# Attention phases of a two-layer encoder: TensorE kept in the order of the code, and projection steps spread 1.3 : 0.1 : 1.7

## The chip, the cores and the metric

The kernel runs on one NeuronCore of one Trainium2 chip. The metric is device time in microseconds (us) of one launch. Of the kernel before, three runs are shown: 2111.12, 2111.41 and 2112.37 us, so the median is 2111.41 us.

## The reference, cut to what matters

Two layers are computed over 1024 tokens of width 1024. The token mixer differs (windowed attention with 12 query heads and 4 key/value heads in layer 0, neighbourhood attention with 12 heads in layer 1); beside it, each layer has 4 heads of cross-attention into 256 memory tokens.

```python
for i in range(DEPTH):                       # DEPTH = 2
    h = rmsnorm(x, norm_mix[i])
    proj = h @ (w_in_a if i % 2 == 0 else w_in_b)      # q, k, v, q_mem
    y_tok = windowed_gqa(q, k, v, sink) if i % 2 == 0 else neighbourhood_attn(q, k, v, rpb)
    y_mem = softmax(q_mem @ k_mem^T * 64**-0.5) @ v_mem
    x = x + concat(y_tok, y_mem) @ w_out[i]
    h = rmsnorm(x, norm_ffn[i])
    gu = h @ w_gate_up[i]
    x = x + (silu(gu[..., :D_FF]) * gu[..., D_FF:]) @ w_down[i]
return rmsnorm(x, norm_final)
```

Every product is made of three fp32r matmuls (high x high, high x low, low x high), which is why each operand is split into a high and a low part.

## The kernel before, in words

**What the attention phase consists of.** Each layer has 16 heads (12 token heads and 4 memory heads), and each head is worked on in two halves of 512 queries, so there are 32 halves, in the order memory heads 0 and 1, token heads 0 to 5, memory heads 2 and 3, token heads 6 to 11. Below, half 0 is the first of a layer. A half (class `Half`, L713) has three jobs:

- `scores` (L739): four query blocks of 128. For each, two matmuls (K high, K low) write a PSUM bank named S; then VectorE and ScalarE read it. For a token head, VectorE adds the bias and takes the maximum in one instruction (L758), which frees the bank, and ScalarE makes the exponential (L762). For a memory head, VectorE takes the maximum (L753) and ScalarE reads the same bank for the exponential (L754), so the bank is free only after both. At the end GpSimd scales the four blocks p (L776).
- `turn` (L784): for each of the four blocks two or three transpositions on TensorE into a PSUM bank named pT (L791), which ScalarE and VectorE copy out as a high part ph and a low part pl (L107 and L110, helpers that serve all splits).
- `mix` (L800): 4 or 10 matmuls on ph and pl into the one bank O (L812), which ScalarE and VectorE copy into y (L822, L833).

PSUM has two banks for S, three that pT shares with the transpositions of V (`vtr`, L596), one for O, and two for the projections (mm, po). So the third block of a half's scores waits until the first block's bank has been read, and the fourth transposed block until the first one's has been copied.

**The projections between.** The input projections of the heads to come are units of two halves of 8 steps (`other_units`, L894); a step is one call of `pull` and issues three 512-column matmuls (L141). After the last unit the same calls bring steps of the output projection, with the tile po (`out_units`, L948). The main loop (L966) goes over the halves. In round i it traces `scores` of half i+1, `mix` of half i-1 and `turn` of half i, and after each block it adds rate/13 to a credit; each whole credit is one `pull`. The rate is what the most urgent unit needs to be done half a round before it is due; once the units are done, it is read from PACE (L37): 0, 2, 4, 4, 4 for the last five rounds.

**What sets the order.** The code is traced in one order, but the instructions of each engine are then put in order by a scheduler, which may move a matmul ahead of others that are traced before it when it reckons that one to be ready sooner. Softmax work and the copies of pT are raised in priority; projection steps are not. So the order in which the code writes TensorE's work is not the one that it runs in.

## Time and profile before

| what | value |
|---|---|
| median of three runs | 2111.41 us |
| the profiled execution's own time | 2112.72 us |
| its span, first to last instruction | 2110.9 us |
| TensorE, matmul busy | 2092.0 us, 99% of the span |
| TensorE, weight loads busy | 1751.5 us, 83% |
| VectorE busy | 1524.3 us, 72% |
| ScalarE busy | 1076.9 us, 51% |
| GpSimd busy | 582.7 us, 28% |

The two attention phases lie at about 75 to 320 us (layer 0) and 1040 to 1390 us (layer 1) of the span; the rest is the memory projections and the feed-forward parts, which the change does not touch. In the profile PE is TensorE's matmul row and PEld its weight loads, DVE is VectorE, ACT ScalarE, POOL GpSimd, SP SyncE. Each matmul has its own weight load. The busy time of a matmul is longer than the distance to the next one's start, since matmuls are pipelined; the distance between starts is what a matmul costs in a stream. In the views by source line the idle time before an instruction is put down to what ended it; "issue" is idle time that ends with no such event.

### The profile page before, as it was taken

To read this page: it belongs to the slowest core of one execution; us is meant where nothing else is said; L and a number is where in the kernel's file an instruction comes from. 1 tells how busy PE (TensorE), PEld (TensorE's weight loads), DVE (VectorE), ACT (ScalarE), POOL (GpSimd) and SP (SyncE) were. 2 spreads that over 40 slices of the span, in tenths; PEclk is the share of its full clock that TensorE was granted. 3 is DMA by queue.
4 is the path that set the end of the run, shared out by engine and by line. 5 is a ranking of instruction groups with operands and counts; after the bars stand their busy time and mean duration, and the time that the engine had idled before them with its cause. 6 is when DMAs were issued, how large, how long until landed. Compare 5 with 4: busy or idle time off the path is not lost.

```text
span 2110.9 us, 29032 instructions
## 1 busy us (share of the span) xinstructions
PE 2092.0 (99%) x10318; PEld 1751.5 (83%) x10318; DVE 1524.3 (72%) x2474; ACT 1076.9 (51%) x2037; POOL 582.7 (28%) x615
## 2 busy tenths in 40 slices
PE   9999999999999999999999999999999999999998
PEld 8788888888888888888888888888788888888886
DVE  7787886897666666866766666677986666678675
ACT  6687785544334335444466666664543434344443
POOL 0344330334434430000233223203343444400001
PEclk9999999999999999999999999999999999999999
DMA  6421138232333227956232222274233333277562
GB/s 233 146 82 51 31 103 283 89 115 101 109 115 110 85 105 281 337 180 206 80 98 68 69 72 78 65 269 155 75 110 105 110 115 105 91 263 280 184 210 94
DMA packets 121776, 288.07 MB, mean 136 GB/s; under 512 B 12704, under 2 KB 21152, under 8 KB 121632
## 3 DMA queue, kind: packets, MB, share of 16 engines
q1 hardware_dynamic: 113744, 272.42, 38.5%
q10 hardware_dynamic: 7888, 13.79, 1.7%
q8 instruction: 82, 1.34, 0.3%
q14 instruction: 62, 0.51, 0.1%
HBM read 211.19 MB, written 68.95 MB: 133 GB/s over the span
## 4 chain that ended last, share of the span: by engine, by line
PE 80%; issue 12%; DVE 3%; POOL 2%; ACT 2%; DMA 1%; SPq 0%; POOLq 0%; ACTq 0%; DVEq 0%
PE X L1104 16%; PE Y L1104 16%; PE mm L141 15%; PE po L141 8%; PE X L1542 5%; PE Y L1542 4%; PE S L746 3%; PE O L812 3%; PE pT L791 3%; PE X L1186 2%; PE Y L1186 2%; PE mm L448 1%; POOL wS L1061 1%; POOL wf L110 1%; DVE wgu L110 0%
## 5 line engine op out<-in xcount | busy, mean ns | idle before, releaser
L1104 PE MATMUL Y<-hB,wgu 128*128 128x512 f32 x1056 | 255.6, 391 | 0.8 <-ACT c L1124 0.8
L1104 PE MATMUL X<-hB,wgu 128*128 128x512 f32 x1056 | 254.9, 391 | 0.0
L1542 PE MATMUL X<-hB,wd 128*128 128x512 f32 (+1 forms) x1092 | 242.9, 383 | 0.0
L110 DVE TENSOR_TENSOR wgu<-wS,wgu 128x1024 fp32r<-128x1024 f32 (+1 forms) x124 | 154.3, 1245 | 120.5 <-ACT wgu L107 120.4
L1542 PEld LDWEIGHTS X<-hB,wd 128*128 128x128 f32 x1092 | 200.2, 188 | 40.1 <-issue 0.5
L1104 PEld LDWEIGHTS Y<-hB,wgu 128*128 128x128 f32 x1056 | 196.8, 188 | 43.4 <-ACT c L1124 1.6
L1104 PEld LDWEIGHTS X<-hB,wgu 128*128 128x128 f32 x1056 | 195.9, 188 | 40.1 <-ACT g L1121 0.2
L776 POOL TENSOR_SCALAR p<-p,stat 128x384 f32<-128x384 f32 (+1 forms) x256 | 141.8, 573 | 302.5 <-DVE stat L773 196.7
L141 PE MATMUL mm<-hT,wqk 128*128 128x512 f32 x672 | 199.2, 405 | 0.0
L107 ACT CAST wgu<-wS 128x1024 fp32r<-128x1024 f32 (+1 forms) x124 | 114.3, 923 | 141.9 <-POOL wS L1061 124.5
L141 PE MATMUL po<-yT,wo 128*128 128x512 f32 x768 | 183.5, 394 | 0.0
L1542 PE MATMUL Y<-hB,wd 128*128 128x512 f32 x792 | 180.2, 389 | 0.0
L1542 PEld LDWEIGHTS Y<-hB,wd 128*128 128x128 f32 x792 | 148.7, 188 | 30.8
L244 POOL TENSOR_TENSOR nr<-nv,neg_half 128x4 f32<-128x4 f32 (+1 forms) x12 | 13.2, 1103 | 582.6 <-DVE nv L243 573.3
L141 PEld LDWEIGHTS po<-yT,wo 128*128 128x128 f32 x768 | 142.9, 188 | 29.1 <-DVE yT L110 0.2
L107 ACT CAST hB<-b_raw 128x512 fp32r<-128x512 f32 x154 | 89.7, 618 | 124.9 <-DMA b_raw<-b_d 108.0
L1104 PE MATMUL X<-hT,wgu 128*128 128x512 f32 x624 | 150.3, 391 | 0.0
L1061 POOL TENSOR_TENSOR wS<-wgu_raw 128x512 f32<-128x512 f32 x44 | 61.1, 1389 | 291.6 <-DVE wgu L110 291.6
L1104 PEld LDWEIGHTS X<-hT,wgu 128*128 128x128 f32 x624 | 116.9, 188 | 26.2
L762 ACT ACTIVATE p<-p,stat 128x256 f32<-128x256 f32 (+1 forms) x192 | 112.3, 586 | 48.7 <-DVE stat L758 47.1
L110 DVE TENSOR_TENSOR hB<-b_raw,hB 128x512 fp32r<-128x512 f32 x154 | 100.3, 689 | 49.8 <-ACT hB L107 49.6
L110 DVE TENSOR_TENSOR pl<-pT,ph 128x384 fp32r<-128x384 f32 (+1 forms) x256 | 119.2, 493 | 17.5 <-ACT ph L107 14.3
(201 smaller groups left out, 4248.3 us busy)
## 6 DMA issues: line engine op xcount, KB each, us to landing
wgu_raw<-in_w_gu SPq DMA_DIRECT2D x92, 512.0 KB, 3.6
b_raw<-b_d SPq DMA_DIRECT2D x70, 512.0 KB, 4.5
wd_raw<-in_w_dn SPq DMA_DIRECT2D x50, 512.0 KB, 4.5
b_d<-c SPq DMA_DIRECT2D x88, 256.0 KB, 2.1
b_d<-t SPq DMA_DIRECT2D x66, 256.0 KB, 2.2
wo_raw<-in_w_out SPq DMA_DIRECT2D x32, 512.0 KB, 3.7
wd_other<-in_w_dn SPq DMA_DIRECT2D x20, 512.0 KB, 7.3
xr_d<-x ACTq DMA_DIRECT2D x32, 256.0 KB, 2.9
```

The lines of the kernel that those rows point to most:

```text
L107: return nc.scalar.copy(dst, src)
L110: return (eng or nc.vector).tensor_tensor(dst, src, h.bitcast(F32), op=ALU.subtract)
L141: nc.tensor.matmul(ps[:, :n], l, r, start=start and i == 0 and j == 0, stop=stop and i == len(order) - 1 and j == 2,)
L746: nc.tensor.matmul(s_[:, :n], Q[self.h][:, qb * P : (qb + 1) * P], k, start=j == 0, stop=j == 1)
L762: nc.scalar.activation(p[:, :n], p[:, :n], AF.Exp, bias=m1, scale=-1.0, accum_out=s1)
L776: nc.gpsimd.tensor_scalar(p[:, :n], p[:, :n], ri[:, i : i + 1], 1.0, op0=ALU.mult, op1=ALU.mult)
L791: nc.tensor.transpose(tr[:, j * P : (j + 1) * P], p[:, j * P : (j + 1) * P], ident)
L812: nc.tensor.matmul(o[:, c0 : c0 + w * P], self.value(j), t[:, s0 : s0 + w].rearrange("p j q -> p (j q)"), start=j == js[0] and t is self.p ...
L1061: sub = lambda o, p_, q_: nc.gpsimd.tensor_tensor(o, p_, q_, op=ALU.subtract)
L1104: nc.tensor.matmul(ps, l, r, start=n in (0, 1, 3, 6) and k == 0 and i == 0, stop=k == 3 and i == 2, skip_group_check=True,)
L1186: nc.tensor.matmul(bank[:, at : at + h2], l, r, start=start and k == 0 and i == 0, stop=stop and k == 1 and i == 2, skip_group_check=True,)
L1542: nc.tensor.matmul(bank[:, c], l, r, start=i in (0, 1, 3, 6) and p == 0 and n == 0, stop=p == HF - 1 and n == 2, skip_group_check=True,)
```

## The change

Three things are changed, all in the attention phases. First, while the main loop runs (a flag `in_order`), every TensorE instruction of the projections, scores, transpositions and mixes is pinned behind the TensorE instruction traced before it. Pinning sets the order of issue only; it adds no wait for a result. Second, the credit that a block adds is weighted by its job: 1.3 for a block of `scores`, 0.1 for a step of `mix`, 1.7 for a block of `turn`. Third, the rate aims a little earlier: 0.7 in place of 0.5 rounds before the due round, with a floor of 0.4 in place of 0.5. No arithmetic and no transfer is added or removed; the number of matmuls of each kind is the same.

```diff
--- before.py
+++ after.py
@@ -138,11 +138,16 @@
         for i, k in enumerate(order):
             terms = three(wk(w, k), (h[k][:, 0, :n], h[k][:, 1, :n]))
             for j, (l, r) in enumerate(terms):
-                nc.tensor.matmul(
+                pe(nc.tensor.matmul(
                     ps[:, :n], l, r, start=start and i == 0 and j == 0,
                     stop=stop and i == len(order) - 1 and j == 2,
-                )
+                ))
             yield
+
+    in_order = [False]
+
+    def pe(ins):
+        return tc.keep_in_program_order(ins) if in_order[0] else ins
 
     def run(g):
         for _ in g:
@@ -593,7 +598,7 @@
                     tr = ps_t.tile([P, HS], F32, tag="T", name="vtr")
                     for b in range(4):
                         c = (4 * u + b) * P
-                        nc.tensor.transpose(tr[:, b * P : (b + 1) * P], vt[:, c : c + P], ident)
+                        pe(nc.tensor.transpose(tr[:, b * P : (b + 1) * P], vt[:, c : c + P], ident))
                     for i in range(2):
                         s_ = tr.rearrange("p (b i d) -> p b i d", b=4, i=2)[:, :, i]
                         hi(vs[i][:, 4 * u : 4 * u + 4, 0], s_)
@@ -743,9 +748,9 @@
                     for i, (qb, b0, b1, n) in enumerate(self.blocks):
                         s_ = ps_s.tile([P, HS], F32, tag="S", name="S")
                         for j, k in enumerate(self.keys(b0, b1)):
-                            nc.tensor.matmul(
+                            pe(nc.tensor.matmul(
                                 s_[:, :n], Q[self.h][:, qb * P : (qb + 1) * P], k, start=j == 0, stop=j == 1
-                            )
+                            ))
                         p = ap.tile([P, 3 * P], F32, tag="p", bufs=8, name="p")
                         m1, s1 = nm[:, i : i + 1], sm[:, i : i + 1]
                         with tc.high_priority(offset=40):
@@ -788,7 +793,7 @@
                     for p, (qb, b0, b1, n) in zip(self.p, self.blocks):
                         tr = ps_t.tile([P, HS], F32, tag="T", name="pT")
                         for j in range(b1 - b0):
-                            nc.tensor.transpose(tr[:, j * P : (j + 1) * P], p[:, j * P : (j + 1) * P], ident)
+                            pe(nc.tensor.transpose(tr[:, j * P : (j + 1) * P], p[:, j * P : (j + 1) * P], ident))
                         s0 = self.slot(b0, qb)
                         sl = slice(s0, s0 + step * (b1 - b0 - 1) + 1, step)
                         src = tr[:, :n].rearrange("p (j q) -> p j q", q=P)
@@ -809,12 +814,12 @@
                         s0, w = self.slot(j, qbs[0]), len(qbs)
                         c0 = (qbs[0] - 4 * u) * P
                         for t in (self.ph, self.pl):
-                            nc.tensor.matmul(
+                            pe(nc.tensor.matmul(
                                 o[:, c0 : c0 + w * P], self.value(j),
                                 t[:, s0 : s0 + w].rearrange("p j q -> p (j q)"),
                                 start=j == js[0] and t is self.ph, stop=j == js[-1] and t is self.pl,
                                 skip_group_check=True,
-                            )
+                            ))
                         yield
 
                     t = temp("yt")
@@ -963,6 +968,7 @@
                 if is_a:
                     pull()
             groups = 13
+            in_order[0] = True
             for i in range(len(halves)):
 
                 rate = 0.0
@@ -970,7 +976,7 @@
                     if done[0] > n:
                         continue
                     left = (n + 1 - n0) * 2 * NK - taken[0]
-                    rate = max(rate, left / max(dues[n] - i - 0.5, 0.5))
+                    rate = max(rate, left / max(dues[n] - i - 0.7, 0.4))
                 if tail is not None:
                     rate = PACE[layer][i - len(halves)]
                 if i == 0:
@@ -981,16 +987,16 @@
                         spread_bias(r)
                 jobs = []
                 if i + 1 < len(halves):
-                    jobs.append(halves[i + 1].scores())
+                    jobs.append((1.3, halves[i + 1].scores()))
                 ahead = halves[min(i + 3, len(halves) - 1)].h
                 if not isinstance(ahead, tuple) and ahead not in biases:
                     biases[ahead] = make_bias(ahead)
                 if i > 0:
-                    jobs.append(halves[i - 1].mix())
-                jobs.append(halves[i].turn())
-                for job in jobs:
+                    jobs.append((0.1, halves[i - 1].mix()))
+                jobs.append((1.7, halves[i].turn()))
+                for share, job in jobs:
                     for _ in job:
-                        credit += rate / groups
+                        credit += share * rate / groups
                         while credit >= 1.0:
                             credit -= 1.0
                             pull()
@@ -1001,6 +1007,7 @@
                 at[0] = i + 1
                 if done[0] == len(units) and tail is None:
                     tail = work = out_units()
+            in_order[0] = False
             for _ in halves[-1].mix():
                 pull()
             run(tail)
```

Line numbers of the changed kernel are higher: the scores are L751 there, the transpositions L796, the mixes L817. A name ends in the number of its tile. Three places on TensorE follow.

Layer 0, the scores of half 17 (second half of memory head 2): the two banks are used in turn by the blocks S_2423, S_2429, S_2438 and S_2444. Before:

```order
L746 MATMUL S_2423<-mKL_1646,QS_1643 128x256
L746 MATMUL S_2429<-mKH_1645,QS_1643 128x256
L746 MATMUL S_2429<-mKL_1646,QS_1643 128x256
L141 MATMUL mm_2398<-hT_586,wv_1804 128x512 x3
L812 MATMUL O_2455<-ph_2379,V_833 128x128
L812 MATMUL O_2455<-pl_2380,V_833 128x128
L141 MATMUL mm_2398<-hT_624,wv_1804 128x512
L746 MATMUL S_2438<-mKH_1645,QS_1643 128x256
L746 MATMUL S_2438<-mKL_1646,QS_1643 128x256
L141 MATMUL mm_2398<-hT_624,wv_1804 128x512
L746 MATMUL S_2444<-mKH_1645,QS_1643 128x256
L746 MATMUL S_2444<-mKL_1646,QS_1643 128x256
```

The same half in the changed kernel, where the blocks are S_2426, S_2435, S_2441 and S_2450:

```order
L751 MATMUL S_2426<-mKH_1593,QS_1591 128x256
L751 MATMUL S_2426<-mKL_1594,QS_1591 128x256
L141 MATMUL mm_2385<-hT_624,wv_1760 128x512 x3
L751 MATMUL S_2435<-mKH_1593,QS_1591 128x256
L751 MATMUL S_2435<-mKL_1594,QS_1591 128x256
L751 MATMUL S_2441<-mKH_1593,QS_1591 128x256
L751 MATMUL S_2441<-mKL_1594,QS_1591 128x256
L141 MATMUL mm_2385<-hT_629,wv_1760 128x512 x3
L751 MATMUL S_2450<-mKH_1593,QS_1591 128x256
L751 MATMUL S_2450<-mKL_1594,QS_1591 128x256
```

Before, the first two blocks are followed by three projection matmuls, two of a mix and one more before the third block. Now the first block is followed by one step of three, then the second and the third block stand back to back, and the third has one step and the second block between it and the block whose bank it takes.

Layer 0, the end of the phase: the transpositions of half 26 (their end, before) and the scores of half 28. Before:

```order
L791 MATMUL pT_3445<-ident_106,p_3305 128x128 x3
L141 MATMUL po_3548<-yT_3269,wo_3254 128x512
L746 MATMUL S_3454<-KH_2838,QS_3104 128x256
L746 MATMUL S_3454<-KL_2839,QS_3104 128x256
L746 MATMUL S_3460<-KH_2838,QS_3104 128x384
L746 MATMUL S_3460<-KL_2839,QS_3104 128x384
L141 MATMUL po_3548<-yT_3269,wo_3254 128x512
L141 MATMUL po_3548<-yT_3274,wo_3254 128x512 x2
L746 MATMUL S_3466<-KH_2838,QS_3104 128x384
L746 MATMUL S_3466<-KL_2839,QS_3104 128x384
L141 MATMUL po_3548<-yT_3274,wo_3254 128x512
L746 MATMUL S_3472<-KH_2838,QS_3104 128x384
```

The same place in the changed kernel:

```order
L796 MATMUL pT_3424<-ident_106,p_3287 128x128 x2
L796 MATMUL pT_3433<-ident_106,p_3293 128x128 x3
L796 MATMUL pT_3439<-ident_106,p_3302 128x128 x3
L796 MATMUL pT_3445<-ident_106,p_3308 128x128 x3
L751 MATMUL S_3454<-KH_2809,QS_3115 128x256
L751 MATMUL S_3454<-KL_2810,QS_3115 128x256
L751 MATMUL S_3460<-KH_2809,QS_3115 128x384
L751 MATMUL S_3460<-KL_2810,QS_3115 128x384
L751 MATMUL S_3466<-KH_2809,QS_3115 128x384
L751 MATMUL S_3466<-KL_2810,QS_3115 128x384
L751 MATMUL S_3472<-KH_2809,QS_3115 128x384
L751 MATMUL S_3472<-KL_2810,QS_3115 128x384
```

Before, steps of the output projection (po) stand between these blocks; now the four transposed blocks and the four blocks of scores follow each other with nothing between.

Layer 1, the scores of half 13, of a token head. Before:

```order
L746 MATMUL S_11129<-KH_10590,QS_10589 128x384
L746 MATMUL S_11129<-KL_10591,QS_10589 128x384
L141 MATMUL mm_11070<-hT_9631,wqk_10674 128x512 x3
L746 MATMUL S_11138<-KH_10590,QS_10589 128x384
L746 MATMUL S_11138<-KL_10591,QS_10589 128x384
L141 MATMUL mm_11160<-hT_9357,wqm_10861 128x512 x3
L746 MATMUL S_11164<-KH_10590,QS_10589 128x384
L746 MATMUL S_11164<-KL_10591,QS_10589 128x384
L746 MATMUL S_11170<-KH_10590,QS_10589 128x256
L746 MATMUL S_11170<-KL_10591,QS_10589 128x256
```

The same half in the changed kernel:

```order
L751 MATMUL S_11161<-KH_10515,QS_10514 128x384
L751 MATMUL S_11161<-KL_10516,QS_10514 128x384
L141 MATMUL mm_11136<-hT_9413,wqm_10815 128x512 x3
L751 MATMUL S_11170<-KH_10515,QS_10514 128x384
L751 MATMUL S_11170<-KL_10516,QS_10514 128x384
L141 MATMUL mm_11136<-hT_9418,wqm_10815 128x512 x3
L751 MATMUL S_11179<-KH_10515,QS_10514 128x384
L751 MATMUL S_11179<-KL_10516,QS_10514 128x384
L141 MATMUL mm_11136<-hT_9426,wqm_10815 128x512 x3
L751 MATMUL S_11188<-KH_10515,QS_10514 128x256
L751 MATMUL S_11188<-KL_10516,QS_10514 128x256
```

Before, the third and fourth block stand back to back; now a projection step of three matmuls stands between any two blocks.

## The prediction

> **What bounds the kernel now.** I read the page's busy shares first, then the windows of the two attention phases beside a window of the feed-forward part, then, for those phases, the idle time before the instructions of single source lines, and last the timeline at some of these waits.
>
> ```profile
> PE 2092.0 (99%) x10318; PEld 1751.5 (83%) x10318; DVE 1524.3 (72%) x2474; ACT 1076.9 (51%) x2037; POOL 582.7 (28%) x615
> ```
>
> ```profile
> core 0: us, PE busy (x) PEld busy (x) DVE busy (x) ACT busy (x) POOL busy (x), PEclk, DMA share, GB/s
> 75.00:320.00 245.00, 241.42 (x1373) 204.61 (x1372) 195.12 (x506) 187.61 (x505) 99.15 (x170) 1.00 0.24 76
> 1040.00:1390.00 350.00, 349.19 (x1869) 293.79 (x1868) 231.60 (x537) 223.08 (x546) 102.05 (x164) 1.00 0.28 83
> 500.00:600.00 100.00, 100.00 (x498) 84.95 (x497) 64.88 (x84) 37.90 (x56) 40.46 (x31) 1.00 0.29 100
> ```
>
> TensorE is the bound everywhere: its matmul row fills 99% of the span at a granted clock of 1.00. The change moves no work off it and adds none, so only time in which TensorE stands still can change, and only in the two windows. They are not alike: VectorE is busy 195.12 of 245 us (80%) in layer 0, but 231.60 of 350 us (66%) in layer 1. The next rows say where TensorE's weight loads sat idle (us, times). Before transpositions (L791) in layer 0 up to 250 us, in layer 0 from 250 to 320 us, and in layer 1 up to 1350 us:
>
> ```profile
>   POOL p L776: 5.4, 12
>   issue: 1.7, 6
>   DVE pl L110: 1.3, 4
> ```
>
> ```profile
>   POOL p L776: 3.0, 7
>   issue: 0.8, 3
> ```
>
> ```profile
>   issue: 1.9, 5
>   POOL p L776: 1.0, 2
> ```
>
> Before scores (L746) in layer 0 up to 250 us and in layer 1 up to 1350 us, and before the transpositions of V (L596) in layer 1:
>
> ```profile
>   ACT p L754: 1.6, 6
>   DVE stat L758: 1.5, 7
> ```
>
> ```profile
>   DVE stat L758: 1.7, 8
>   DMA KL<-KL: 0.5, 1
> ```
>
> ```profile
>   ACT vT L639: 0.9, 4
> ```
>
> All of it is some 20 us. That is what is at stake in either direction: the best order can win a part of it, a worse one can add waits of the same kinds.
>
> By the busy row the two phases leave 245 - 241.42 and 350 - 349.19, 4.4 us together. The Trainium skill (Perfetto Trace Analysis, Identifying the Most-Contended Engine) says that matmul occupancy is a bad measure of the room left and that the busy share of weight loads is a better one; by it the phases lie at 83.5% and 83.9%, the feed-forward window at 84.95%, which leaves about 3.5 + 3.6 = 7 us (an estimate). By the first measure a gain of 6 us, the rival below, has no room; by the second it just has. The idle rows agree with the second.
>
> **The waits that the new order brings.** A memory head's scores take a bank that VectorE and then ScalarE must have read. This is the timeline in layer 0 where the third block waits for the first:
>
> ```profile
> 200.13 0.28 PE L746 MATMUL S<-mKL,QS 128*128 128x256 f32 x1
> 200.50 0.86 PE L141 MATMUL mm<-hT,wv 128*128 128x512 f32 x3
> 200.55 0.75 DVE L753 TENSOR_REDUCE stat<-S 128x1 f32<-128x256 f32 x2
> 201.06 0.47 ACT L754 ACTIVATE p<-S,stat 128x256 f32<-128x256 f32 x1 [0.94 <-DVE stat L753]
> 201.20 0.22 PE L812 MATMUL O<-ph,V 128*128 128x128 f32 x1
> 201.53 0.47 ACT L754 ACTIVATE p<-S,stat 128x256 f32<-128x256 f32 x1
> 201.68 0.19 PEld L746 LDWEIGHTS S<-mKH,QS 128*128 128x128 f32 x1 [0.18 <-ACT p L754]
> 201.68 0.38 PE L746 MATMUL S<-mKH,QS 128*128 128x256 f32 x1
> 201.90 0.28 PE L746 MATMUL S<-mKL,QS 128*128 128x256 f32 x1
> ```
>
> Three matmuls of 512 columns take 201.20 - 200.50 = 0.70, and of 256 columns 0.12 each (200.13 to 200.50 is three). The first block's second matmul starts at 200.13, VectorE's maximum at 200.55, ScalarE's exponential at 201.06, and the bank is free for the third block at 201.68: 1.55 after 200.13. In the changed order (half 17 in the section on the change) the third block, or the one that follows a step, comes 0.12 + 0.70 + 0.24 = 1.06 after. It would wait 0.49; VectorE's two maxima here run as one row of 0.75, and with the first at half of that and started at once the chain is about 0.15 shorter, which gives 0.34. I take 0.43. After such a wait the second matmul comes 0.22 after the first (201.68, 201.90) in place of 0.12, so 0.10 more.
>
> On that 0.10 the Trainium skill (TensorE: Matmul & The Clock Gate, Step-by-step) says that TensorE pulls weight loads ahead of matmuls in flight while matmuls keep program order. In the row, the waiting block's load starts at 201.68 with its matmul, not ahead. By the rule the 0.10 would vanish from some 23 waits, about 2.3 us less in the sum, 2113.7; the row decides, and I keep it.
>
> Counting in the new order: in layer 0, seven halves of memory heads have one such wait, and two of them (scores as two blocks, a step, two blocks) a second of about 0.2 for the fourth block: 7 x 0.43 + 2 x 0.2 + 9 x 0.10 = 4.3, less the 1.6 of row "ACT p L754" that goes: **+2.7** (bounds 1.7 and 3.5, with 0.34 and 0.49).
>
> A token head's bank is free after VectorE alone:
>
> ```profile
> 131.31 0.34 PE L746 MATMUL S<-KL,QS 128*128 128x384 f32 x1
> 131.80 0.62 DVE L758 CUSTOM_DVE_ANT_0 p<-S,bias,nsink 128x384 f32<-128x384 f32 x1 [0.28 <-PE S L746]
> 132.38 0.62 DVE L758 CUSTOM_DVE_ANT_0 p<-S,bias,nsink 128x384 f32<-128x384 f32 x1
> ```
>
> With VectorE free, the bank is read 132.38 + 0.1 - 131.31 = 1.17 after the block's second matmul, the next block's 0.58 later. Three blocks' paces (0.18 + 0.70 + 0.35 = 1.23) just cover it. Of 24 halves of token heads in layer 0, 12 now go two blocks, a step, two blocks. There the fourth block starts 0.35 after the third, while its bank comes 0.58 after: 0.2 lost. And VectorE is not always free:
>
> ```profile
> 1139.20 0.34 PE L746 MATMUL S<-KL,QS 128*128 128x384 f32 x1
> 1139.24 0.69 DVE L110 TENSOR_TENSOR QS<-mm,QS 64x512 fp32r<-64x512 f32 x1
> 1140.58 0.19 PEld L746 LDWEIGHTS S<-KH,QS 128*128 128x128 f32 x1 [0.42 <-DVE stat L758]
> ```
>
> Here a copy of 0.69 is ahead, and the block waits until 1.38 after 1139.20. I take 0.25 + 0.10 for the 12 halves, and 0.05 for eight others that go one block, step, two blocks, step: 4.6, less the 1.5 of row "DVE stat L758" in layer 0: **+3.1**. If all is hidden it is -1.5; with the copy ahead each time (0.5 and 0.16) it is +5.8.
>
> At the start of layer 1 the scores of half 0 lose the transpositions and steps that stood between their blocks (0.67 and 0.24 between freeing and use, where 1.4 is wanted), and half 1 is like the memory halves above: 0.7 + 0.6 + 0.4 + 0.3 for restarts = **+2.0** (0.8 to 2.6).
>
> The end of layer 0: halves 28 and 29 now have no projection step at all, since the units end earlier and the first PACE entry is 0. What VectorE needs for a half:
>
> ```profile
> L110 DVE TENSOR_TENSOR pl<-pT,ph 128x384 fp32r<-128x384 f32 (+1 forms) x256 | 119.2, 493 | 17.5 <-ACT ph L107 14.3
> L758 DVE CUSTOM_DVE_ANT_0 p<-S,bias,nsink 128x384 f32<-128x384 f32 (+1 forms) x96 | 53.1, 580 | 4.3 <-PE S L746 3.0 <-PE O L812 0.3 <-PE pT L791 0.2
> L833 DVE TENSOR_TENSOR y<-O,yt 64x512 f32<-64x512 f32 x64 | 43.6, 682 | 41.0 <-ACT yt L822 40.2
> ```
>
> 4 x 0.580 + 4 x 0.493 + 0.682 = 4.97 us. TensorE needs about 3.8 us (an estimate: 5632 columns at 0.23 per 512, and eleven transpositions taken as 256-column matmuls). So 1.2 us is lost in each of the two, and the splits of the output weights stand on VectorE at the same place (the 1.51 us row below). The lists give some 2.3 us of loss there now; I take 4.3, **+2.0**. If the copies ahead are worked off in the gap, all of the 2.3 goes; with the splits on top, +5.
>
> V's transpositions follow the last step of their unit at once when pinned, six units in all: the copy that they wait for has 0.44 to 0.76 us of cover where now it has 0.67 to 1.0: **+1.0** (-0.9 to +2).
>
> **The waits that it takes away.** The fourth transposed block waits for a bank:
>
> ```profile
> 255.98 1.51 DVE L110 TENSOR_TENSOR wo<-wo_raw,wo 128x1024 fp32r<-128x1024 f32 x1 [0.27 <-ACT wo L107]
> 257.41 1.97 DVE L110 TENSOR_TENSOR pl<-pT,ph 128x384 fp32r<-128x384 f32 x4
> 258.10 0.41 PE L791 MATMUL pT<-ident,p 128*128 128x128 f32 x2 [0.55 <-DVE pl L110]
> ```
>
> A 1.51 us split held VectorE, the four copies pl came late, and TensorE stood for 0.55. With the share 1.7 a step of 0.70 now stands between the blocks, so that nearly everywhere a bank has 2.03 us from its last transposition to its next use, where 1.57 was common. The 8.4 us in layer 0 up to 250 us are 22 waits; less 0.15 each, which the matmul ahead still covers, 5.1 are lost. Their mean is 0.38, below the 0.46 gained, but some are 0.8: I take **-3.5** (0 to -5.1). In layer 1, 2.9 us in 7 waits, so 1.9 lost: **-1.0** (0 to -1.9). There scores now have a step between all blocks (1.9 given against 1.17): of the 1.7 us "DVE stat" I take **-1.2** (0 to -1.7). K arrives earlier, since units end 0.2 rounds earlier: **-0.5** (0 to -0.5) for the DMA row. The transfers are the same ones on the same queue (SP), issued at the same steps, and no other wait for one stands in the rows.
>
> **The sum:** 2.7 + 3.1 + 2.0 + 2.0 + 1.0 - 3.5 - 1.0 - 1.2 - 0.5 = +4.6 us. Made against the profiled execution (span 2110.9, own time 2112.72) this is 2117.3; that execution lies 1.3 above the median of 2111.41, so I predict **2116.0 us**, slower by 0.22%.
>
> **The rivals.** All start from the median.
>
> *The waits go, the new ones are covered* (faster). For: time in which TensorE waits for a bank of scores is time in which VectorE and ScalarE catch up, so a later transposition finds its bank; layer 1 has 34% of VectorE free. Against: the new distances in layer 0 are below the measured chain. All of -5.1, -1.9, -1.7 and -0.5, half of the tail's 2.3, and half of 5.8 for the scores: -10.4 + 2.9 + 1.0 = -6.5, **2104.9 us**. Its point: the third block's wait in layer 0 stays below 0.2 us.
>
> *The waits only move* (no change). For: VectorE at 80% in layer 0; what it is late with at a transposition, it is late with at a score. Layer 0 then comes to 0 and layer 1 to 2.0 + 0.5 - 2.7 = -0.2: **2111.2 us**.
>
> *The end of layer 0 starves* (slower still). For: two halves without steps on a full VectorE. Against: its transfers and splits are asked for earlier. Tail +5, token heads +5.8: 2.7 + 5.8 + 2.0 + 5.0 + 1.0 - 3.5 - 1.0 - 1.7 = +10.3, **2121.7 us**.
>
> That the order is not changed is ruled out by the instruction order shown.
>
> **How the numbers follow.** A measurement of this kernel can tell about 0.2% (4.2 us) from none, so faster is below 2107.2 and slower above 2115.6. Forecast 0.40 (own range 2113 to 2120: 0.29 slower, 0.11 same), the faster rival 0.26 (0.25 faster, 0.01 same), the wash 0.20 (0.18 same, 0.02 slower), the starving end 0.14 (slower). So faster 0.25, same 0.30, slower 0.45. All bounds at once would span about 2100 to 2130; both ends need every unknown to fall the same way, so I take 2104 to 2125.
>
> **What would show it.** Right: more idle before L751 with "ACT p" and "DVE stat" as releasers in layer 0 (about 6 us more), less before L796 with "POOL p" and "DVE pl" (8.4 to under 4), a gap of 1 to 2 us twice between 250 and 265 us, and almost none before scores in layer 1. Wrong: memory scores in layer 0 that start without a wait, or idle before L796 that stays.

## The result, and the profile after

The changed kernel takes **2144.85 us** (median of 5, 2142.86 to 2145.90), the kernel before in the same comparison 2111.41 (2110.62 to 2113.45): a ratio of 1.0157, with a 95% interval of 1.0146 to 1.0169. The change costs 33.4 us. The prediction was 2116.0 with a range up to 2125: the right sign and a seventh of the size. The profiled execution took 2145.9 us with a span of 2144.1.

The page's busy shares, and the windows of the two attention phases (columns as in the prediction's windows; the phase of layer 1 now lies from 1060 to 1420 us), of the changed kernel:

```profile
PE 2100.7 (98%) x10318; PEld 1756.3 (82%) x10318; DVE 1528.4 (71%) x2474; ACT 1083.6 (51%) x2037; POOL 579.8 (27%) x615
75.00:320.00 245.00, 229.02 (x1273) 190.40 (x1272) 185.19 (x485) 179.84 (x486) 94.40 (x165) 0.99 0.19 60
1060.00:1420.00 360.00, 346.44 (x1843) 292.95 (x1842) 229.81 (x529) 220.51 (x539) 101.81 (x164) 0.98 0.26 78
```

The matmuls are the same 10318, and VectorE and ScalarE have as much to do as before. In layer 0 TensorE is busy 229.02 of 245 us where it was 241.42, and the granted clock is no longer 1.00. A view by source line adds up the idle time of both rows of TensorE, weight loads and matmuls, so a wait that empties both is counted twice. The rows of idle time from here on are of the weight loads alone. Before the scores (L751), in layer 0 up to 260 us (TensorE is then about as far in its work as at 250 before), from 260 to 325, and in layer 1 up to 1385:

```profile
  DVE stat L763: 7.4, 21
  ACT p L759: 6.2, 11
```

```profile
  DVE stat L763: 8.7, 11
```

```profile
  ACT p L759: 4.7, 7
  DVE stat L763: 1.8, 6
```

Before the transpositions (L796) in layer 0 up to 260 us, and before the mixes (L817) from 260 to 325 us:

```profile
  POOL p L781: 2.4, 6
  issue: 0.6, 2
```

```profile
  ACT stat L774: 1.8, 1
  DVE y L838: 1.1, 1
```

The waits of the transpositions went down, as forecast: 7.2 to 3.0 us for the weight loads alone, 8.4 to 3.5 with both rows. The waits of the scores grew from 3.1 to 13.6 us in the same stretch (before, only the weight loads had any). At the end of the layer the mixes wait longer for their one bank, 2.9 us where it was 1.4, and now the matmul row stands still as well (1.52 us in the timeline below); the prediction had no term for that.

**Where the 33 us lie.** All kernels here do the same matmuls. I gave each matmul the interval between starts that is usual for its shape (512 columns 0.229 us, 384 0.1745, 256 0.1185, 128 0.059, a transposition 0.109), called what an interval has above this lost, and added the lost time up by how far TensorE's work has come, so that kernels line up. Lost us in the profiled executions (the last four columns belong to experiments below):

| place | before | changed | pin_only | steps_free | free_ends | free_both |
|---|---|---|---|---|---|---|
| layer 0, first 25 us | 1.8 | 5.0 | 7.8 | 1.5 | 5.1 | 1.5 |
| layer 0, middle | 9.8 | 14.2 | 30.9 | 8.9 | 13.5 | 9.0 |
| layer 0, end | 4.3 | 15.7 | 20.9 | 11.9 | 6.1 | 5.6 |
| layer 1, start | 1.0 | 7.7 | 7.0 | 2.5 | 7.6 | 1.6 |
| layer 1, middle | 5.8 | 4.6 | 10.0 | 4.2 | 4.6 | 4.2 |
| layer 1, end | 3.8 | 14.5 | 14.3 | 9.1 | 3.7 | 3.8 |
| sum | 26.5 | 61.7 | 90.9 | 38.1 | 40.6 | 25.7 |
| span | 2110.9 | 2144.1 | 2178.5 | 2121.8 | 2124.4 | 2109.5 |

The sums differ as the spans do, within 3.2 us. Against before, the ends of the two phases cost 11.4 + 10.7, the start of layer 1 6.7, layer 0 ahead of its end 7.6, and only the middle of layer 1 gained, 1.2.

**The end of layer 0.** TensorE's timeline in the changed kernel, then VectorE's:

```profile
291.50 0.34 PE L751 MATMUL S<-KH,QS 128*128 128x384 f32 x1
291.68 0.34 PE L751 MATMUL S<-KL,QS 128*128 128x384 f32 x1
293.92 0.45 PE L751 MATMUL S<-KH,QS 128*128 128x384 f32 x1 [1.91 <-DVE stat L763]
...
294.21 0.34 PE L751 MATMUL S<-KL,QS 128*128 128x384 f32 x1
...
296.60 0.47 PE L817 MATMUL O<-ph,V 128*128 128x256 f32 x1 [1.52 <-DVE y L838]
```

```profile
289.00 1.23 DVE L110 TENSOR_TENSOR wo<-wo_raw,wo 128x1024 fp32r<-128x1024 f32 x1 [0.26 <-ACT wo L107]
290.33 1.50 DVE L110 TENSOR_TENSOR pl<-pT,ph 128x256 fp32r<-128x256 f32 x3
292.91 0.56 DVE L110 TENSOR_TENSOR pl<-pT,ph 128x384 fp32r<-128x384 f32 x1 [1.08 <-ACT ph L107]
293.38 0.47 DVE L763 CUSTOM_DVE_ANT_0 p<-S,bias,nsink 128x256 f32<-128x256 f32 x1
```

Two blocks of scores stand in their banks at 292.0, but VectorE has its last copy `pl` ahead of them, and that waits 1.08 for ScalarE. Only at 293.38 is the first block read, and TensorE stands 1.91 us with nothing else allowed. Then the mix stands 1.52 for its bank, whose drain (L838) is behind the maxima of the scores. From 286 to 304 us TensorE is busy for 12.28 of 18 us, VectorE for 12.82 and ScalarE for 11.54 (the row is shown below): no engine is the bound, the round goes around as one chain. The same place before the change shows what the scheduler did there with the same work:

```profile
290.48 0.48 PE L141 MATMUL po<-yT,wo 128*128 128x512 f32 x1
290.80 0.28 PE L746 MATMUL S<-KH,QS 128*128 128x256 f32 x1
290.91 0.28 PE L746 MATMUL S<-KL,QS 128*128 128x256 f32 x1
291.19 0.52 PE L791 MATMUL pT<-ident,p 128*128 128x128 f32 x3
291.47 0.71 PE L141 MATMUL po<-yT,wo 128*128 128x512 f32 x2
```

It broke the steps into single matmuls and put them, scores and transpositions between one another.

**The end and the start of layer 1.** TensorE's timeline at both places, changed kernel:

```profile
1383.09 1.04 PE L796 MATMUL pT<-ident,p 128*128 128x128 f32 x8
1387.15 0.52 PE L796 MATMUL pT<-ident,p 128*128 128x128 f32 x3 [3.03 <-POOL p L781]
1390.76 0.58 PE L751 MATMUL S<-KH,QS 128*128 128x256 f32 x1 [3.08 <-DMA KH<-KH]
1393.62 0.58 PE L751 MATMUL S<-KL,QS 128*128 128x256 f32 x1 [2.29 <-DMA KL<-KL]
```

```profile
1078.69 1.28 ACT L759 ACT_TABLE_LOAD   x1
1079.99 0.47 ACT L759 ACTIVATE p<-S,stat 128x256 f32<-128x256 f32 x1
1080.61 0.38 PE L751 MATMUL S<-mKH,QS 128*128 128x256 f32 x1 [1.93 <-ACT p L759]
```

At the end, the transpositions wait for a late softmax, then the last head's scores wait for the two transfers of its K, one after the other. At the start, the first exponential follows a weight split and the loading of ScalarE's function table, 1.28 us. The same two places in the kernel before:

```profile
1360.19 2.79 PE L141 MATMUL po<-yT,wo 128*128 128x512 f32 x11
1366.23 0.45 PE L746 MATMUL S<-KH,QS 128*128 128x256 f32 x2
```

```profile
1059.92 2.46 PE L141 MATMUL mm<-hT,wqk 128*128 128x512 f32 x10
1060.11 1.28 ACT L754 ACT_TABLE_LOAD   x1
```

Before, eleven matmuls of the output projection and more behind them run until the last head's scores, and ten projection matmuls run while the table is loaded.

**The clock.** Windows of the changed kernel, cut where the granted clock changes (the column after POOL's is the clock):

```profile
283.03:286.44 3.41, 1.90 (x8) 1.02 (x7) 3.13 (x10) 2.77 (x8) 0.46 (x1) 1.00 0.22 77
286.44:289.86 3.42, 3.32 (x13) 3.32 (x14) 2.61 (x6) 2.51 (x6) 1.89 (x4) 0.50 0.00 0
289.86:293.27 3.41, 1.84 (x14) 1.31 (x12) 2.18 (x5) 2.87 (x6) 1.29 (x2) 1.00 0.00 0
293.27:296.68 3.41, 1.24 (x5) 0.71 (x6) 3.09 (x11) 2.57 (x9) 0.00 (x0) 1.00 0.00 0
296.68:300.10 3.42, 3.42 (x15) 3.42 (x16) 0.92 (x4) 0.84 (x4) 2.16 (x4) 0.50 0.00 0
1078.33:1081.75 3.42, 1.49 (x10) 1.09 (x9) 2.22 (x4) 3.39 (x7) 0.35 (x1) 1.00 0.06 13
1081.75:1085.16 3.41, 3.41 (x10) 2.66 (x9) 2.93 (x7) 2.35 (x9) 1.77 (x4) 0.50 0.65 187
```

After a block of 3.41 us in which TensorE was busy for 1.90, 1.24 or 1.49 us, the next whole block runs at 0.50, though TensorE is busy through most of it. After the one with 1.84 us it does not; the last section says what sets it apart. With the three blocks from 1388.95 to 1399.19, TensorE was busy 16.3 us in all at half the rate; half of that, up to 8 of the 33 us (an estimate from these rows), is what the waits cost beyond themselves. How much of it the time pays is open: in pace0 below, no block at the end of layer 0 runs at 0.50, and that end lost only 1.4 us less. Nothing of this kind is in the attention phases of the kernel before, where the clock is 1.00.

### The profile page after: what moved, and what is told of

It reads as the page before. It is cut to its first block, busy times and chain, and to the rows that moved or that the text cites. A ratio compares the mean times of both kernels' runs of the same rounds, so it can differ in the third digit from the quotient of the medians.

```text
span 2144.1 us, 29033 instructions
## 1 busy us (share of the span) xinstructions
PE 2100.7 (98%) x10318; PEld 1756.3 (82%) x10318; DVE 1528.4 (71%) x2474; ACT 1083.6 (51%) x2037; POOL 579.8 (27%) x615
## 4 chain that ended last, share of the span: by engine, by line
PE 78%; issue 12%; DVE 4%; ACT 3%; POOL 2%; DMA 1%; POOLq 0%; ACTq 0%; DVEq 0%; SPq 0%
PE X L1111 16%; PE Y L1111 16%; PE mm L141 14%; PE po L141 8%; PE X L1549 5%; PE Y L1549 4%; PE O L817 4%; PE S L751 3%; PE pT L796 3%; PE X L1193 2%; PE Y L1193 2%; PE mm L453 1%; DVE pl L110 1%; POOL wS L1068 1%; POOL wf L110 1%
```

## The experiments

All times are medians, with the ratio to the kernel before measured beside them; the changed kernel is 2144.85 us throughout. The kernel before lay between 2111.17 and 2112.76 us beside the different groups of runs, so a difference of 1 to 2 us between two experiments says little. "Free" means not pinned.

**pin_only: pinned, with the old shares and aim.**

```diff
-                    jobs.append((1.3, halves[i + 1].scores()))
+                    jobs.append((1.0, halves[i + 1].scores()))
-                    jobs.append((0.1, halves[i - 1].mix()))
+                    jobs.append((1.0, halves[i - 1].mix()))
-                jobs.append((1.7, halves[i].turn()))
+                jobs.append((1.0, halves[i].turn()))
-                    rate = max(rate, left / max(dues[n] - i - 0.7, 0.4))
+                    rate = max(rate, left / max(dues[n] - i - 0.5, 0.5))
```

> The traced order is kept, but the projection steps are spread evenly (1 : 1 : 1) and the aim of the rate is the old one. Theory A (the loss sits in the places where pinned instructions stand behind something that is late: the ends of both phases and the start of layer 1, about 13 + 10 + 6 us): these places do not depend on the shares, so most of the +33 us stays, 2135 to 2150 us. Theory B (the loss comes from the new distances between blocks of scores, which the shares 1.3 : 0.1 : 1.7 make): with even shares the distances return and the kernel comes to within 8 us of before, 2111 to 2119 us.

Measured: 2176.99 us, ratio 1.0306 (1.0290 to 1.0321). Neither theory: pinning alone costs 64.6 us against 2112.42 measured beside it, and the shares and the new aim bring back half of it, 32 (no run separates the two). The idle rows of the weight loads before the scores, layer 0 up to 260 us:

```profile
  DVE stat L763: 12.4, 20
  ACT p L759: 7.9, 11
```

That is 20.3 us where the changed kernel has 13.6, and before the transpositions stand another 11.7, 3.0 in the changed kernel, though this run is about 15 us less far in its work at 260 us. Theory B is wrong in its sign: the new distances are better than even ones, for scores and transpositions both.

**shares_only: new shares and aim, nothing pinned.**

```diff
-            in_order[0] = True
```

> The shares and the new aim stay, nothing is pinned: the scheduler may move TensorE's instructions as in the kernel before. Theory A: within 4 us of before, 2108 to 2116 us, since the scheduler fills a late place with other matmuls. Theory B (distances made by the shares): 2125 to 2145 us.

Measured: 2114.7 us, ratio 1.0010 (1.0000 to 1.0019). As theory A has it: with the scheduler free, the shares and the aim hardly matter. All of the loss but some 2 us hangs on the pinning.

**free_ends and middles: where the pinning costs.** `free_ends` frees rounds 26 to 31 of each layer, `middles` rounds 0 and 1 too.

```diff
-            in_order[0] = True
             for i in range(len(halves)):
+                in_order[0] = i < len(halves) - 6          # free_ends
+                in_order[0] = 2 <= i < len(halves) - 6     # middles
```

> The changed kernel, but from half 26 of each layer on nothing is pinned. Theory A: the 13 us at the end of layer 0 and the 10 us at the end of layer 1 go, most of them: 2121 to 2126 us. Theory B (waits for banks all over both phases): the ends are 12 of 64 halves, so 5 to 7 of 33 us go: 2137 to 2141 us.

> As with the ends free, and rounds 0 and 1 of each layer not pinned either. Theory A: the 6 us at the start of layer 1 go too, some of the 5 in layer 0 remain, layer 1's middle stays 2.5 better than before: 2113 to 2120 us. Theory B: 2135 to 2140 us.

Measured: free_ends 2125.47 us, ratio 1.0062 (1.0047 to 1.0077), 19.4 us less than the changed kernel; middles 2121.98 us, ratio 1.0045 (1.0029 to 1.0062). Theory A's places hold: in the table the two ends fall to 6.1 and 3.7, near before. In middles the 1.93 us gap at the first exponential of layer 1 is gone from the trace as well. Middles came out 2 us above what theory A gave, with 9.6 us still lost against before. In its profile some 4 of these lie in the middle of layer 0, which is still pinned, and some 3 behind that layer, where one block of the clock, from 406.7 us, ran at 0.50.

**steps_free: everything in the traced order but the projection steps.**

```diff
             for j, (l, r) in enumerate(terms):
-                pe(nc.tensor.matmul(
+                nc.tensor.matmul(
```

> The changed kernel, but the projection steps are not pinned: scores, O and transpositions keep the traced order among themselves, the steps may fall where the scheduler finds room. Theory C (pinning costs because the only work on TensorE that waits for nothing, the steps, can no longer fill a late place): most of the 33 us goes, 2112 to 2120 us. Theory D (the order among scores, O and transpositions itself is what waits): little goes, 2135 to 2145 us.

Measured: 2122.81 us, ratio 1.0054 (1.0039 to 1.0069). Two thirds of the loss is gone, some 3 us short of what theory C gave. In the table the start and middle of layer 0 are back at 1.5 and 8.9, the start of layer 1 at 2.5. The idle rows of the weight loads before its scores, layer 0 up to 260 us, with 13.6 us in the changed kernel:

```profile
  DVE stat L763: 4.9, 19
  ACT p L759: 1.6, 7
```

What remains lies at the two ends, 11.9 and 9.1, where few steps are left.

**free_both: steps free everywhere, and everything free from round 26 on.** Both edits above together.

> The changed kernel with the projection steps free throughout and nothing pinned from half 26 of each layer on. If the loss is the sum of the two causes (pinned steps in the body of the phases, the order of scores, O and transpositions where few steps are left), it comes to steps_free less what its profile still loses at the two ends against before, 7.6 and 5.3 us: 2122.8 - 12.9 = 2110, at most 2 us off before. If a third cause is left: 2115 us or more. A gain over before of 2 us or more would be new.

Measured: 2111.86 us, ratio 0.9998 (0.9989 to 1.0007). The sum holds, no third cause shows, and there is no gain over before. It is the fastest version with pinning, and it is the kernel before in time.

**early_k and early_k2: the transfers of the last K.**

```diff
             dues = [due(*n) for n in names]
+            dues[-1] -= layer               # early_k
...
             for i in range(len(halves)):
+                if i == 24:                 # early_k2
+                    dues[-1] -= layer
```

> The changed kernel, but in layer 1 the last unit (Q and K of head 11) is due one round earlier, so that K's two transfers have a round more. Theory K (the 10 us at the end of layer 1 come from the two transfers, 3.1 and 2.3 us of waiting, and from the low granted clock behind them): both waits go, 7 to 9 us less, 2136 to 2138 us. Theory E (the end of a phase starves for any reason: without these waits TensorE waits for VectorE and ScalarE at the same place): at most 3 us less, 2142 to 2146 us.

> The changed kernel; the last unit of layer 1 is due one round earlier, as in early_k, but the due time changes only at round 24, so that the rate of the rounds before stays as it is. In early_k the profile lost 5.0 us less at the end of layer 1 and 2.7 more between 1100 and 1300 us of TensorE work. Theory K: with the rounds before as they were, the 5 us show: 2138 to 2141 us. Theory E: what is saved at K's transfers is lost again in the rounds that now have no steps: 2143 to 2146 us.

Measured: early_k 2144.2 us, ratio 1.0155 (1.0140 to 1.0170); early_k2 2142.02 us, ratio 1.0142 (1.0129 to 1.0156). The waits for both transfers are gone from both traces. What stands at the place in early_k2:

```profile
1381.70 0.41 PE L796 MATMUL pT<-ident,p 128*128 128x128 f32 x2 [1.51 <-DVE pl L110]
...
1386.62 0.30 PE L817 MATMUL O<-ph,V 128*128 128x128 f32 x1 [1.83 <-DVE y L838]
```

So 5.4 us of waiting for K was worth 0.7 us in early_k, where theory E put it, and 2.8 us in early_k2, between the theories (their profiles lost 5.0 and 4.0 less at that end). K's round trip was the last of several late things, and without it the round waits for VectorE as at the end of layer 0. The whole of 10.7 us cannot be put down to the transfers.

**pace0 and no_split: what the end of layer 0 waits for.**

```diff
-PACE = [0, 2, 4, 4, 4], [0, 2, 4, 4, 4]
+PACE = [1, 3, 3, 3, 4], [0, 2, 4, 4, 4]                    # pace0
-                                wo[m] = load_w(a["w_out"][layer, m], name="wo")
+                                wo[m] = load_w(a["w_out"][layer, m], name="wo") if layer or m == 0 else wo[0]
-                wo[2] = load_w(a["w_out"][layer, 2], name="wo")
+                wo[2] = load_w(a["w_out"][layer, 2], name="wo") if layer else wo[0]   # both: no_split
```

> The changed kernel with the 14 steps of the output projection at the end of layer 0 spread 1, 3, 3, 3, 4 over the last five rounds, not 0, 2, 4, 4, 4. Theory F (the rounds without a step between scores, O and transpositions are what waits there): 4 to 6 us of the 12 at the end of layer 0 go, 2139 to 2141 us. Theory G (the splits of the output weights on VectorE and ScalarE are what waits, and the steps wait for them too): within 2 us of 2145, or slower.

> The changed kernel; in layer 0 the output weights 1 and 2 are left out (weight 0 is used in their place), so that two of the three splits at the end of layer 0, 1.0 us on ScalarE and 1.2 to 1.5 us on VectorE each, and their loads fall away. Theory G: 3 to 6 us less, 2139 to 2142 us. Theory F: at most 2 us less, 2143 to 2146 us.

Measured: pace0 2145.91 us, ratio 1.0166 (1.0149 to 1.0183); no_split 2142.51 us, ratio 1.0148 (1.0133 to 1.0163). Pace0 lies where theory G put it: moving the same few steps among the last rounds does nothing, and theory F falls. No_split leaves out two of the three splits and comes out between the two ranges: they are worth 2.3 us of the 11.4, where theory G gave 3 to 6. In their profiles that end lost 1.4 and 3.7 us less. The splits add to the chain; with two of three gone, most of the loss is still there.

**s_free, t_free, st_free, p_free, ts_free: which order at the ends.** From round 26 on, one or two kinds are free, the rest pinned: scores (s), transpositions of p (t), steps (p), or both letters.

```diff
-    def pe(ins):
-        return tc.keep_in_program_order(ins) if in_order[0] else ins
+    def pe(ins, end=True):
+        return tc.keep_in_program_order(ins) if in_order[0] and (end or not late[0]) else ins
...
+                late[0] = i >= len(halves) - 6
...
-                            pe(nc.tensor.transpose(tr[:, j * P : (j + 1) * P], p[:, j * P : (j + 1) * P], ident))
+                            pe(nc.tensor.transpose(tr[:, j * P : (j + 1) * P], p[:, j * P : (j + 1) * P], ident), end=False)
```

> The changed kernel, but from half 26 of each layer on the scores alone are not pinned; O, transpositions and steps keep their order. Freeing everything there brought 19.4 us. Theory H (the scores stand first in the round, wait for a bank or for K, and hold up O and transpositions that are ready): 13 us or more of it comes back, 2126 to 2132 us. Theory I (the transpositions wait for the softmax, and the scores of the next half stand behind them): under 6 us, 2139 to 2145 us.

> The changed kernel, but from half 26 of each layer on the transpositions of p alone are not pinned. Theory I: 13 us or more of the 19.4 come back, 2126 to 2132 us. Theory H: under 6 us, 2139 to 2145 us. If both kinds alone bring 6 to 12 us, the wait is a ring through both.

> The changed kernel, but from half 26 of each layer on the projection steps alone are not pinned; scores, O and transpositions keep their order. Theory J (at the ends too the steps are the filler that is missing): steps_free, in which they are free in all rounds, lost 9 us less at the two ends than the changed kernel, so 2135 to 2138 us. Theory R (each kind waits for the next in a ring, and steps alone can't break it): 2141 to 2146 us.

> The changed kernel, but from half 26 on transpositions and steps are not pinned; scores and O keep their order between them. If the two add up (7 from the transpositions, 9 from the steps): 2128 to 2131 us. If the pair is the whole cause: 2124 to 2127 us, as with everything free. If they break the same wait: 2135 to 2138 us.

> The changed kernel, but from half 26 on scores and transpositions are not pinned; O and steps keep their order between them. If scores matter once the transpositions can move: 2124 to 2132 us. If scores never matter: 2136 to 2139 us, as with the transpositions alone.

| free at the ends | us | ratio to before | less than changed |
|---|---|---|---|
| scores | 2143.88 | 1.0151 (1.0138 to 1.0165) | 1.0 |
| transpositions | 2138.11 | 1.0123 (1.0110 to 1.0137) | 6.7 |
| scores, transpositions | 2136.81 | 1.0115 (1.0100 to 1.0130) | 8.0 |
| steps | 2133.62 | 1.0105 (1.0087 to 1.0124) | 11.2 |
| transpositions, steps | 2126.57 | 1.0072 (1.0055 to 1.0089) | 18.3 |
| everything (free_ends) | 2125.47 | 1.0062 (1.0047 to 1.0077) | 19.4 |

Theory H falls: freeing the scores, before which the longest waits stand, brings nothing measurable, alone or beside the transpositions. The transpositions alone fall between theories H and I, and the steps alone bring 1.4 us more than theory J allowed. Transpositions and steps together give, within the noise, all that freeing everything gives, and their single gains add up to it (6.7 + 11.2 = 17.9). A wait is shown at the instruction that stands, but the time came from the others that could have run meanwhile. Windows from 286 to 304 us of the changed kernel and of ts_free:

```profile
286.00:304.00 18.00, 12.28 (x57) 10.45 (x58) 12.82 (x31) 11.54 (x31) 5.77 (x9) 0.81 0.00 1
```

```profile
286.00:304.00 18.00, 17.35 (x106) 14.55 (x104) 16.18 (x46) 15.34 (x45) 7.41 (x12) 1.00 0.00 1
```

With TensorE fed, VectorE also does 16.18 us of work in these 18 where it did 12.82: it had not been too slow, it had been waiting in the same ring. And the clock stays at 1.00.

## Why the prediction was wrong

**What was right.** TensorE is the bound, and nearly all that changed is its idle time in the attention phases; the rest is the clock, below. The sign was right, in part by luck: the sum was +10.8 of new waits against -6.2 of old ones, and most of the loss came at places for which it had little or nothing. "pT waits layer 0 -3.5" is borne out: 8.4 us of idle rows became 3.5. The price of a restart, 0.10, is about what it was: after the wait that ends at 293.92 the second matmul follows 0.29 later (294.21), 0.17 being usual. The rival "the end of layer 0 starves" named one of the right places.

**The step that failed first: "that is what is at stake in either direction", some 20 us.** The waits of the kernel before were taken as the measure of what an order can lose. They bound what can be won. They say nothing of what a worse order adds, since before the change the scheduler hid lateness by moving a transposition or a few matmuls of a step into the gap, and a hidden wait leaves no row. The prediction priced where the steps go, and never priced that they can go nowhere else: pinning alone is 64.6 us, and the shares, which the prediction charged with +2.7 and +3.1 for the scores, are together with the aim a gain of 32 once the order is pinned.

**Memory and token heads' scores in layer 0: +2.7 and +3.1, mis-sized.** The idle time of the weight loads before them grew by 10.5 us, 3.1 to 13.6, where the prediction gave about 6 more. (It called its rows those of the weight loads, but the view counts both rows of TensorE: of the 8.4 us before transpositions, 7.2 are weight loads'. And with 0.34 and 0.49 its sum for memory heads has bounds of 2.1 and 3.1, not 1.7 and 3.5. Neither changes the forecast by much.) The chain of a bank was costed with VectorE or ScalarE free, or with one copy of 0.69 ahead. The trace has more ahead:

```profile
163.81 1.04 ACT L107 CAST wqq<-wqq_raw 128x1024 fp32r<-128x1024 f32 x1
...
164.88 1.24 ACT L107 CAST ph<-pT 128x384 fp32r<-128x384 f32 x3
...
165.39 1.49 DVE L110 TENSOR_TENSOR pl<-pT,ph 128x384 fp32r<-128x384 f32 x3 [0.58 <-ACT ph L107]
...
166.80 0.47 DVE L763 CUSTOM_DVE_ANT_0 p<-S,bias,nsink 128x256 f32<-128x256 f32 x1
...
167.33 0.44 PE L751 MATMUL S<-KH,QS 128*128 128x384 f32 x1 [0.42 <-DVE stat L763]
```

A weight split of 1.04 delays three copies on ScalarE, these delay three on VectorE, and the scores' bank is read after all of them. Here each engine passes its lateness on to the next. On balance layer 0 lost 3.2 + 4.4 ahead of its end; the prediction's own terms there, with -3.5 for the transpositions, come to +2.3.

**The end of layer 0: +2.0 with +5 as its bound, measured +11.4.** The step compared what VectorE needs for a half (4.97 us) with what TensorE needs (3.8), as if both ran without a stop. They run in turn: scores, VectorE, ScalarE, GpSimd, transpositions, copies, mixes, with one bank for O and two for scores. The windows show VectorE idle 29% of 286 to 304 us. A difference of loads was the wrong model; the length of the ring was the right one.

**The end of layer 1: no term, measured +10.7.** The sum had "K arrives earlier -0.5" for transfers. In TensorE's work the last unit did end a little earlier, by 0.7 us. But K's first transfer was issued 6.4 us after the unit's last matmul (1381.46 and 1387.88), where it had been 4.3 (1358.59 and 1362.88), and K's scores were now the next instruction that TensorE was allowed, while before they had been moved behind projection work. early_k2 gives up to 2.8 of it to the transfers; ts_free and free_ends show that the rest goes when transpositions and steps can move.

**The start of layer 1: +2.0, measured +6.7.** The prediction counted the distances between the blocks, but the bank waits for an exponential behind a 1.05 us split and a 1.28 us table load, which stood in the trace of before without TensorE standing still. That wait is 1.93, and the block at 0.50 behind it, in which TensorE is busy for 3.41, costs up to 1.7 more.

**"pT waits layer 1" -1.0 and "layer-1 scores" -1.2.** The middle of layer 1 gained 1.2 of these 2.2. The first came: the transpositions' idle time fell from 2.9 to 1.6 us. The second did not: weight loads of the scores wait 1.8 us for VectorE after, 1.7 before.

**The clock: no term.** Waits were priced at their length; the blocks at 0.50 behind them cost up to 8 us more.

**V's transpositions, +1.0,** are not separable from the rest here; their weight loads' idle time in layer 1 grew from 0.9 to 1.7 us.

## What to carry to other kernels

When an edit fixes an order that a scheduler was free to choose, the rows of waits before the edit are what was left after the scheduler's repairs: ask of each late engine what would run in its place, and price the places with the least independent work (starts, ends, a rare table load) first. Where such an order is wanted, leave the work that waits for nothing, here the projection steps, out of it, and let the ends go free: here that only brought back the time of the kernel before. Before pricing an idle gap at its length, add up how much of the clock's block it empties.

## What the runs showed of the hardware

The granted clock moves in blocks of 3.41 us, and one block that is only partly filled is enough to halve the next. The seventeen profiles of this case, without the last 25 us of each, have 10,385 blocks at full speed. Sorted by busy time, all 23 in which TensorE was busy for up to 45.5% were followed by a block at 0.50; of the 69 from 45.7% to 71%, 12 were; of the 10,293 above, none. The line is sharper when each matmul counts with the interval that is usual for its shape (the same ones as above; for other shapes in proportion to the columns) in place of its busy time, which is longer than that: of 34 blocks filled to less than 40%, all were followed by one at 0.50; of 3 between 40% and 41.7%, one; of the 10,348 above, none. This sets the rows of the section on the result apart: the block with 1.90 us busy is filled to 37%, the one with 1.84 us to 43%. So a gap of some 2 us that lies within one block, or several that add up to it, can cost up to 1.7 us more.

The Trainium skill (TensorE: Matmul & The Clock Gate, What's actually happening) has the same block of about 3.4 us and the same half rate, but speaks of an idle window. Here TensorE was busy for 1.49 of 3.42 us in the block ahead of 1081.75, and for 1.90 of 3.41 ahead of 286.44: the measurement decides, and partly filled blocks count.

A wait's row names the instruction that stands. It did not tell which instruction to free: the weight loads of the scores sat idle for 8.7 us at the end of layer 0, and freeing them brought 1.0 us at both ends together.
